# Two modulation chunks of the second layer computed at the end of the first layer's experts

## The chip, the cores and the metric

One core of a Trainium2 chip runs the whole program. The metric is the time of one execution in microseconds (us), as the device takes it. Names of engines are those of the profile: PE is the matrix engine and PEld its weight loads, DVE the vector engine, ACT the scalar engine, POOL the GpSimd engine, SP the engine that only issues transfers. A letter q behind an engine is its queue of issues.

## The reference, cut to what matters

Two layers act on 256 context rows and 512 latent rows of width 1024. Each layer makes six modulation vectors ("chunks" 0 to 5, 1024 numbers each) from a conditioning vector, once for the latent rows and once for the context rows:

```
m_lat = jnp.split((sc @ ada_w[i] + ada_b[i])[:, None, :], 6, axis=-1)
m_ctx = jnp.split(scc @ ada_w[i] + ada_b[i], 6, axis=-1)
h_lat = modulate(rms_norm(x, norm_mix_w[i]), m_lat[0], m_lat[1])
...
x = x + m_lat[2].astype(x.dtype) * y_lat
h_lat = modulate(rms_norm(x, norm_ffn_w[i]), m_lat[3], m_lat[4])
...
x = x + m_lat[5].astype(x.dtype) * f[B * L:].reshape(B, S, D)
```

`ada_w[i]` is 1024 by 6144 numbers of 4 bytes, so the weights of one chunk are 4 MB. They depend on nothing that the layers compute. The mixer between chunks 1 and 2 is softmax attention beside a gated delta rule that goes through the rows in 12 steps, forwards and backwards at once. The FFN is a mixture of 32 experts, two per row; each expert has 3 MB of weights.

## The kernel before, in words

Each layer goes through the same stages: norm and transposition of the rows (`norm_mix`, L424, in the second layer); the input projection, in units of columns, with the short convolution and the triangular solve of the delta rule (`layer`, L1593 on, in the order of `ORDER`, L126); the scan of 12 steps with the attention as filling (L1641); the output projection, norm and router (L1694); the experts (`experts`, L1421). A planner that simulates the program settles the order of the instructions on each engine and in each queue. Where `pin` (L163) is used, the order is that of the text.

**Modulation.** `ada_steps` (L271) makes one chunk in four parts; a part (`ada_part`, L257) loads 1 MB of `ada_w` by POOL's queue into one of two buffers (L231), multiplies it in eight matmuls of 128x32 by 128x256 on four column strips of PE (L265; the profile shows each as two records), and adds the result to a sum (ACT L267 for the first, DVE L269 for the others). After the fourth the bias is added (L282) and the chunk is written to a small array in DRAM, `md` (POOL's queue, L283). The scan calls a part for each letter a in `PAT` (L130), an attention slot for each f and a piece of the delta step for each d. In the second layer each of the 12 steps has two letters a, and there are 16 parts (chunks 2 to 5), so steps 0 to 7 have two each and the last four steps none. On PE the order of this stage is pinned.

**Experts.** Of an expert's weights, w1 and w3 (2 MB together) go into one of four buffers `w13` of 16 KB per partition (`RB`, L98; L1317), w2 into one of two buffers `w2`, all by SP's queue and three experts ahead (`LA`). Expert e multiplies in `expert_up` (L1362, L1364), turns the result (L1380), multiplies by w2 (L1406), scales (DVE L1413) and adds the rows into `yd` by an indirect transfer of POOL's (L1418). Each such addition waits for the one before it. After expert 31 there is a branch (L1503) for rows that overflow, and then the second layer begins: SP loads the rows x from `yd` (L1751), ACT squares them (L326), PE transposes (L343), `norm_chunks` makes the operands `nT`, `hh` and `hl` (L345 to L350).

**Memory.** The tiles of a stage lie in stacked pools. A tile that takes the place of older tiles waits until all work on those is done. In the second layer the pool "nm" of the norm begins with `nT` (24 KB per partition); when it closes, the pool "pp" of the projection begins at the same address with `gev` (L1558), which takes the first projected unit (c0 = 2560) from PSUM (`gate`, L1010). Three PSUM tiles of tag "a" hold such results (`PSA`, L111). In the first layer the `w13` buffers lie where the second layer has `hh`, `hl`, its first weights `wraw` (L231, the part on SP's queue) and the small table `wqk` (L444).

Of the kernel before, what the change touches and what calls it, by code (L numbers as in the profile page):

```python
# [13 lines left out]
F32 = mybir.dt.float32  # L14
# [115 lines left out]
PAT = (('fdfdfffdfffafddffffdfaffdfd', 'fdfffdffdfdfafddffdfafffdfaf', 'fdffdfffdfdfafddffdfafffdff'), ('fdffdffadffdfddafdffdf', 'fdffdffadffdfddafdffdf', 'fdffdffddadffdfadd'))  # L130
WB = 2
LA, E0 = 3, 2
QUEUE = dict(w="sync", ada="gpsimd", att="gpsimd", step="sync", idd="sync", iud="sync", ild="sync", iy="sync", ix="sync", qk="sync", qg="scalar", vk="scalar", h2="scalar", se="gpsimd", res="scalar")
# [11 lines left out]
class Model:  # L145
# [97 lines left out]
    def cond(self):  # L243
# [6 lines left out]
        nc.vector.tensor_scalar(cc, cc, 0.5, None, op0=OP.mult)  # L250
        sc = self.cp.tile([P, 8, 32], F32, name="scp")
        nc.vector.memset(sc, 0.0)
        nc.vector.scalar_tensor_tensor(sc[:, :, 0:2], th, 1.0, cc, op0=OP.add, op1=OP.mult)
# [17 lines left out]
    def ada_steps(self, i, ch, pool, q):  # L271
# [12 lines left out]
        yield  # L284

    def md_row(self, i, ch, v):

        return self.md[i][ch].rearrange("(o g r) j -> r o g j", o=1, g=4)[v].to_broadcast([P, 4, UNIT])

# [811 lines left out]
    def logit_shift(self, i, v, rw, rb, pool):  # L1101
# [3 lines left out]
        for g in range(4):  # L1105
            nc.sync.dma_start(m[32 * g:32 * g + 32], self.md[i][3][32 * g + v].rearrange("(p k) -> p k", k=8))
        mb = pool.tile([P, 8, P], F32, tag="h2T", bufs=1, name="mb")
# [202 lines left out]
    def expert_load(self, i, e, n, pool):  # L1310
# [13 lines left out]
        return w  # L1324

    def split(self, src, name, pool):

# [92 lines left out]

    def experts(self, i, R, js, g5, h2d, yd, ntok, xw):  # L1421

# [32 lines left out]
        def out(e):  # L1455
            if e >= 0:
                y = self.expert_out(py.pop(e), gates.pop(e), xp)
                self.expert_add(y, col(e), yd, ntok)
# [11 lines left out]
        eo, nb = R["eo"], R["nb"]  # L1470
        xes = []
        self.pins(True)
        for e in range(XE):
# [5 lines left out]
        for e in range(NE):  # L1479
            load(e + LA)  # L1480
            pa = self.psA("pab")
            xt, w, hl = x.pop(e), w13.pop(e), p13.pop(e)
# [13 lines left out]
        turn(NE - 1)  # L1496
        out(NE - 2)
        down(NE - 1)
        out(NE - 1)
        self.pins(False)  # L1500
        assert not list(rest)
# [21 lines left out]
    def layer(self, i, xsrc, rows, done, xstack, mod):  # L1523
# [20 lines left out]
        with self.pool("hp", B) as hp:  # L1544
            with self.pool("pj", B) as wp:
                mp.update(self.rope_params(i, wp))
                first = []
                with self.pool("nm", B) as pool:
                    start = lambda: first.extend(self.wnat(i, 2560, 288, wp))
                    hh, hl = self.norm_first(rows, start, pool, hp) if i == 0 else self.norm_mix(i, rows, start, mod, pool, hp)  # L1550
                done()
                mid = left.enter_context(self.pool("mid", A))
# [73 lines left out]
        with self.pool("at", B) as pool:  # L1626
# [3 lines left out]
            def modulation():  # L1630
                for l, ch in [(i, c) for c in range(2, 6)] + ([(i + 1, 0), (i + 1, 1)] if not last else []):
                    yield from self.ada_steps(l, ch, pool, QUEUE["ada"])
# [47 lines left out]
        nc.sync.dma_start(rb[:, 4:36], t["re_b"][i:i + 1, :].to_broadcast([P, 32]))  # L1680
        rt = self.route_open(T, rp)
        route = lambda n, lg: self.route_pair(rt, n, [tt - t0 for tt in tiles[n:n + 2]], lg, n == T - 2, tl)
        vb, vnow = {nm: tl.tile([P, D], F32, name=nm, tag=nm) for nm in ("g2", "m3", "s4")}, None
# [10 lines left out]
        for n, tt in enumerate(tiles):  # L1694
# [8 lines left out]
            if n == T - 1:  # L1703
                left.close()
                xw = xws.enter_context(self.pool("xw", A))
                ex = self.experts(i, rt, [tt - t0 for tt in tiles], g5, h2d, yd, ntok, xw)
                next(ex)
# [82 lines left out]
```

## Time and profile before

| what | value |
|---|---|
| time, median of 3 runs | 2092.97 us (2085.26 to 2104.73) |
| the profiled execution's own time | 2092.51 us |
| its span, first to last instruction | 2090.7 us |
| mean granted clock of PE, as a share of full speed | 0.902 |
| PE busy | 1763.9 us (84%) |
| DVE busy | 1460.2 us (70%) |
| ACT busy | 1016.6 us (49%) |
| POOL busy | 868.6 us (42%) |
| moved by DMA | 427.81 MB, mean 205 GB/s |

Busy time is the time in which an engine executes; shares are of the span. They are means over stages that have different limits, so the stages have to be read one by one. The experts of the first layer run from about 720 to 1104 us, the second layer's norm and projection from 1110 to about 1400, its scan from about 1460 to 1625, its experts at the end.

### The profile page before, as it was taken

To read this page: it belongs to the slowest core of one execution; us is meant where nothing else is said; L and a number is where in the kernel's file an instruction comes from. 1 tells how busy PE (TensorE), PEld (TensorE's weight loads), DVE (VectorE), ACT (ScalarE), POOL (GpSimd) and SP (SyncE) were. 2 spreads that over 40 slices of the span, in tenths; PEclk is the share of its full clock that TensorE was granted. 3 is DMA by queue.
4 is the path that set the end of the run, shared out by engine and by line. 5 is a ranking of instruction groups with operands and counts; after the bars stand their busy time and mean duration, and the time that the engine had idled before them with its cause. 6 is when DMAs were issued, how large, how long until landed. Compare 5 with 4: busy or idle time off the path is not lost. (4 is left out here: it accounts for less than half of the span.)

```text
span 2090.7 us, 35600 instructions
## 1 busy us (share of the span) xinstructions
PE 1763.9 (84%) x13835; PEld 1382.1 (66%) x13835; DVE 1460.2 (70%) x2472; ACT 1016.6 (49%) x1595; POOL 868.6 (42%) x915
## 2 busy tenths in 40 slices
PE   6998798978877879999996987776898577999994
PEld 4887687766656746666665866675676465777773
DVE  4469996567673668887874579992678465787774
ACT  3444344665541246565554543343566225666663
POOL 4456653234354423343226466650234443334321
PEclk9999897799998979999997998875899788999997
DMA  9222445798645389998853323445983558988872
GB/s 283 74 71 82 129 119 166 218 259 246 205 125 144 147 327 336 332 322 301 324 161 119 97 73 97 131 130 158 282 233 83 148 214 315 346 334 330 328 295 102
DMA packets 227687, 427.81 MB, mean 205 GB/s; under 512 B 83720, under 2 KB 157180, under 8 KB 202939
## 3 DMA queue, kind: packets, MB, share of 16 engines
q1 hardware_dynamic: 171547, 329.09, 47.1%
q0 software_dynamic: 33536, 72.59, 12.2%
q10 hardware_dynamic: 22432, 23.81, 3.3%
q8 instruction: 111, 1.82, 0.4%
q14 instruction: 61, 0.50, 0.1%
HBM read 386.82 MB, written 84.67 MB: 226 GB/s over the span
## 5 line engine op out<-in xcount | busy, mean ns | idle before, releaser
L1418 POOL DMA_INDIRECT yd<-ey,idx x64 | 114.2, 1784 | 425.3 <-DMA yd<-ey,idx 151.8
L1364 PE MATMUL pab<-w,xt 128*128 128x512 f32 x512 | 230.3, 592 | 0.0
L1332 ACT ACTIVATE w2h<-w 128x2048 fp32r<-128x2048 f32 x64 | 122.7, 1917 | 134.5 <-PE py L1406 83.3
L1333 DVE TENSOR_TENSOR w2l<-w,w2h 128x2048 fp32r<-128x2048 f32 x64 | 146.8, 2294 | 53.5 <-ACT w2h L1332 52.9
L1333 DVE TENSOR_TENSOR w13l<-w,w13h 128x2048 fp32r<-128x2048 f32 x64 | 146.5, 2288 | 28.9 <-ACT w13h L1332 28.9
L1364 PEld LDWEIGHTS pab<-w,xt 128*128 128x128 f32 x512 | 93.0, 191 | 92.0 <-issue 91.8
L489 POOL TENSOR_TENSOR wlo<-wraw,whi 128x1024 fp32r<-128x1024 f32 (+1 forms) x44 | 111.1, 2529 | 93.1 <-ACT whi L488 93.1
L239 PE MATMUL pn<-whi,hh 128*128 128x256 f32 (+1 forms) x432 | 134.6, 314 | 16.3 <-ACT gev L1562 12.5
L239 PE MATMUL po<-woh,m 128*128 128x512 f32 x320 | 114.1, 434 | 30.7 <-ACT woh L1069 14.5
L239 PE MATMUL pn<-whi,hl 128*128 128x256 f32 (+1 forms) x432 | 135.3, 316 | 2.0 <-DVE hl L350 1.7
L239 PE MATMUL pn<-wlo,hh 128*128 128x256 f32 (+1 forms) x432 | 132.4, 308 | 1.2 <-POOL wlo L489 1.2
L1332 ACT ACTIVATE w13h<-w 128x2048 fp32r<-128x2048 f32 x64 | 121.8, 1902 | 6.4 <-DMA w<-w 4.1
L239 PE MATMUL pt<-hh,wlo 128*128 128x512 f32 (+1 forms) x352 | 124.2, 353 | 0.0
L239 PE MATMUL pt<-hh,whi 128*128 128x512 f32 (+1 forms) x352 | 122.9, 349 | 0.0
L239 PE MATMUL pt<-hl,whi 128*128 128x512 f32 (+1 forms) x352 | 122.2, 347 | 0.0
L1406 PE MATMUL py<-w2h,gh 128*128 128x512 f32 x256 | 109.1, 426 | 4.6 <-DVE ey L1413 4.4
L1337 POOL DMA_INDIRECT xe<-h2d,idx x64 | 85.9, 1343 | 61.2 <-issue 22.9
L518 DVE SCALAR_TENSOR_TENSOR dT<-xin,cw,dT 128x772 f32<-128x772 f32 x64 | 80.1, 1252 | 43.3 <-ACT dT L516 41.5
L1406 PE MATMUL py<-w2h,gl 128*128 128x512 f32 x256 | 103.1, 403 | 7.8 <-DVE gl L1385 7.8
L1413 DVE TENSOR_TENSOR ey<-py,eg 128x1024 f32<-128x1024 f32 x64 | 78.2, 1222 | 44.1 <-PE py L1406 37.8
L239 PEld LDWEIGHTS pn<-whi,hh 128*128 128x128 f32 x432 | 90.6, 211 | 23.2 <-ACT gev L1562 13.5
L1348 PEld LDWEIGHTS xt<-cst,xe 128*128 128x128 f32 x512 | 68.3, 192 | 55.1 <-issue 29.8
(401 smaller groups left out, 5124.4 us busy)
## 6 DMA issues: line engine op xcount, KB each, us to landing
w<-w SPq DMA_DIRECT2D x192, 1024.0 KB, 9.8
araw<-ada_w POOLq DMA_DIRECT2D x40, 1024.0 KB, 6.8
wraw<-w_in SPq DMA_DIRECT2D x40, 512.0 KB, 4.1
lk<-vk SPq DMA_DIRECT2D x48, 256.0 KB, 7.2
lx<-xad SPq DMA_DIRECT2D x40, 256.0 KB, 10.0
araw<-ada_w SPq DMA_DIRECT2D x8, 1024.0 KB, 10.9
wr<-w_out SPq DMA_DIRECT2D x8, 1024.0 KB, 13.4
vk<-vr ACTq DMA_DIRECT2D x16, 384.0 KB, 3.7
```

Of the source, the lines that this page charges most:

```text
L239: self.nc.tensor.matmul(ps, a(k), b(k), start=(first and n == 0), stop=(last and n == 3 * nk - 1))
L489: getattr(nc, eng).tensor_tensor(lo, raw, hi, op=OP.subtract)
L518: nc.vector.scalar_tensor_tensor(dst, xin[:, tap:tap + 772], cw[:, tap, f:f + 1], dst, op0=OP.mult, op1=OP.add)
L1332: self.pin(nc.scalar.activation(hi, src, AF.Copy))
L1333: self.pin(nc.vector.tensor_tensor(lo, src, hi, op=OP.subtract))
L1337: self.pin(self.nc.gpsimd.indirect_dma_start(out=xe, out_offset=None, in_=h2d, in_offset=bass.IndirectOffsetOnAxis(ap=idx, axis=0), bounds ...
L1348: pin(nc.tensor.transpose(ps[:, k * P:(k + 1) * P], xe.rearrange("p (q k) -> p k q", k=8)[:, 4 * q + k, :], self.ident))
L1364: self.pin(self.nc.tensor.matmul(out, xt[:, k, :], w13[:, :, KS + k, :], start=False, stop=(k == 3)))
L1406: pin(self.nc.tensor.matmul(py[:, n * 512:(n + 1) * 512], a[:, j, :], b[:, c], start=(j + m == 0), stop=(j == 1 and m == 2)))
L1413: pin(nc.vector.tensor_tensor(y, py, gates, op=OP.mult))
L1418: self.pin(self.nc.gpsimd.indirect_dma_start(out=yd, out_offset=bass.IndirectOffsetOnAxis(ap=idx, axis=0), in_=y, in_offset=None, bounds_c ...
```

## The change

The second layer's chunks 2 and 3 (`LATE`) are no longer made in its scan. `experts` of the first layer gets a generator `ada_late`. It loads their 8 MB as four pieces of 2 MB (`half_load`, two transfers of 1 MB each on SP's queue) into `w13` buffers, where experts 32 to 35 would have come, one piece at each of the loop's last three turns and one behind it. Its 64 matmuls go to one PSUM tile: for the second chunk the vector operand is a shifted view of a padded tile (`self.scs`), so that its results fall into rows 2 and 3 of each strip. Eight of the matmuls stand ahead of expert 31's `expert_down` on PE, 56 behind it. ACT then copies the sum to a tile `la` in the pool "rp". In the second layer, `ada_close` opens a pool "lb" when "nm" has closed and before "pp" opens: it loads the two biases by SP's queue, adds them to the sum on DVE and writes two `md` arrays by POOL's queue. `md_row` and `logit_shift` read the second chunk two rows further down. The scan of the second layer has eight parts left (chunks 4 and 5), which fill the letters a of steps 0 to 3.

```diff
+LATE = (2, 3)
...
-        sc = self.cp.tile([P, 8, 32], F32, name="scp")
-        nc.vector.memset(sc, 0.0)
+        pad = self.cp.tile([P, 260], F32, name="scp")
+        nc.vector.memset(pad, 0.0)
+        self.scs = [pad[:, 2 - 2 * j:258 - 2 * j].rearrange("p (k r) -> p k r", k=8) for j in range(2)]
+        sc = self.scs[0]
...
+    def ada_late(self, i, chs, pool, load):
+        if not chs:
+            return
+        acc = self.late_sum = pool.tile([P, UNIT], F32, tag="la", name="la")
+        src = self.t["ada_w"][i].rearrange("(p k) n -> p k n", k=8)
+        raws = []
+        for ch in chs:
+            for n in range(2):
+                raws.append(load(src[:, 4 * n:4 * n + 4, ch * D:(ch + 1) * D]))
+                yield
+        ps = self.psC("aps")
+        for j in range(2):
+            for k in range(8):
+                if k % 2 == 0:
+                    yield
+                for g in range(4):
+                    w = raws[2 * j + k // 4][:, k % 4, g * UNIT:(g + 1) * UNIT]
+                    self.pin(self.nc.tensor.matmul(ps[32 * g:32 * g + 32, :UNIT], self.scs[j][:, k, :], w, start=(j + k == 0), stop=(j == 1 and k == 7), tile_position=(0, 32 * g)))
+        self.pin(self.nc.scalar.activation(acc, ps[:, :UNIT], AF.Copy))
+
+    def ada_close(self, i, chs, pool):
+        for j, ch in enumerate(chs):
+            ab = pool.tile([P, UNIT], F32, tag="lb%d" % ch, name="lb")
+            self.nc.sync.dma_start(ab, self.t["ada_b"][i, ch * D:(ch + 1) * D].rearrange("(g o j) -> g o j", g=4, o=1).to_broadcast([4, 32, UNIT]))
+            self.nc.vector.tensor_tensor(ab, self.late_sum, ab, op=OP.add)
+            getattr(self.nc, QUEUE["ada"]).dma_start(self.md[i][ch], ab)
+            self.mdrow[i, ch] = 2 * j
...
+    def half_load(self, src, pool):
+        w = pool.tile([P, 2, 8, FF], F32, tag="w13", bufs=RB, name="w13").rearrange("p a k f -> p (a k f)").rearrange("p (k n) -> p k n", k=4)
+        for n in range(2):
+            self.nc.sync.dma_start(w[:, 2 * n:2 * n + 2], src[:, 2 * n:2 * n + 2])
+        return w
...
         for e in range(NE):
             load(e + LA)
+            if e + LA >= NE:
+                next(late, None)
...
         turn(NE - 1)
         out(NE - 2)
+        for _ in range(3):
+            next(late, None)
         down(NE - 1)
         out(NE - 1)
+        for _ in late:
+            pass
...
                     hh, hl = self.norm_first(rows, start, pool, hp) if i == 0 else self.norm_mix(i, rows, start, mod, pool, hp)
+                if i > 0:
+                    with self.pool("lb", B) as lb:
+                        self.ada_close(i, LATE, lb)
                 done()
...
-                for l, ch in [(i, c) for c in range(2, 6)] + ([(i + 1, 0), (i + 1, 1)] if not last else []):
+                for l, ch in [(i, c) for c in range(2, 6) if i == 0 or c not in LATE] + ([(i + 1, 0), (i + 1, 1)] if not last else []):
```

## Rows read from the trace of the kernel before

**Rows 1.** The page's slices: GB/s in 40 equal parts of the span.
```profile
GB/s 283 74 71 82 129 119 166 218 259 246 205 125 144 147 327 336 332 322 301 324 161 119 97 73 97 131 130 158 282 233 83 148 214 315 346 334 330 328 295 102
```

**Rows 2.** Second layer's scan, DVE in time: start, duration, engine, line; one per step.
```profile
1520.37 0.68 DVE L921 TENSOR_TENSOR w<-pz,scs 128x512 f32<-128x512 f32 x1
1534.70 0.68 DVE L921 TENSOR_TENSOR w<-pz,scs 128x512 f32<-128x512 f32 x1
1550.92 0.68 DVE L921 TENSOR_TENSOR w<-pz,scs 128x512 f32<-128x512 f32 x1
...
1582.00 0.69 DVE L921 TENSOR_TENSOR w<-pz,scs 128x512 f32<-128x512 f32 x1
...
1593.72 0.68 DVE L921 TENSOR_TENSOR w<-pz,scs 128x512 f32<-128x512 f32 x1
```

**Rows 3.** Modulation parts on PE in time: one at half, one at full clock.
```profile
1417.33 1.94 PE L265 MATMUL aps<-araw,scp 128*32 128x256 f32 x16
...
1524.27 1.07 PE L265 MATMUL aps<-araw,scp 128*32 128x256 f32 x16
```

**Rows 4.** Windows, first experts' end: length, busy (x) of PE/PEld/DVE/ACT/POOL, PEclk, DMA, GB/s.
```profile
1040.00:1050.00 10.00, 10.00 (x43) 6.93 (x42) 9.96 (x9) 6.18 (x7) 3.10 (x2) 1.00 0.98 335
...
1070.00:1080.00 10.00, 9.54 (x41) 6.68 (x40) 9.96 (x9) 7.61 (x10) 1.57 (x1) 1.00 0.43 129
...
1090.00:1100.00 10.00, 7.79 (x27) 5.13 (x26) 4.42 (x7) 0.77 (x2) 3.45 (x2) 0.95 0.19 28
1100.00:1110.00 10.00, 2.97 (x8) 1.78 (x6) 1.42 (x2) 0.22 (x1) 3.47 (x9) 0.67 0.22 29
```

**Rows 5.** SP's queue in time, end of the first experts.
```profile
1061.00 11.21 SPq L1323 DMA_DIRECT2D w<-w  x2
...
1110.56 0.82 SPq L1751 DMA_DIRECT2D x<-yd  x2
```

**Rows 6.** Layer junction in time: PE's last product, last addition, first squares.
```profile
1098.16 0.47 PE L1406 MATMUL py<-w2h,gh 128*128 128x512 f32 x1 [2.21 <-DVE ey L1413]
...
1102.21 0.51 PE L1406 MATMUL py<-w2l,gh 128*128 128x512 f32 x1
...
1105.79 1.54 POOL L1418 DMA_INDIRECT yd<-ey,idx  x1 [5.96 <-issue]
...
1114.08 1.03 ACT L326 ACTIVATE sq<-x 128x1024 f32<-128x1024 f32 x1 [9.39 <-DMA x<-yd]
```

**Rows 7.** End of the second layer's norm in time, on POOL, ACT and PE.
```profile
1146.47 0.73 POOL L350 TENSOR_TENSOR hl<-nT,hh 128x256 fp32r<-128x256 f32 x1 [1.26 <-ACT hh L348]
...
1147.24 0.94 ACT L1010 ACTIVATE gev<-pn 128x256 f32<-128x256 f32 x3 [0.84 <-POOL hl L350]
...
1148.36 0.40 PE L239 MATMUL pn<-whi,hh 128*128 128x288 f32 x1 [0.70 <-ACT ba L1566]
```

**Rows 8.** DMA issues: output<-input, queue, count, KB each, median us to landing.
```profile
yl<-dy SPq DMA_DIRECT2D x24, 128.0 KB, 3.5
...
atd<-fu POOLq DMA_DIRECT2D x8, 256.0 KB, 5.3
...
ab<-ada_b POOLq DMA_DIRECT2D x10, 128.0 KB, 8.3
```

**Rows 9.** A chunk's last steps in the second scan, in time: bias addition and write.
```profile
1514.20 0.42 DVE L282 TENSOR_TENSOR ac<-ac,ab 128x256 f32<-128x256 f32 x1
...
1517.66 0.60 POOL L283 DMA_DIRECT2D md<-ac  x1
```

**Rows 10.** Windows as in Rows 4: the projection after the junction, and the solve.
```profile
1158.00:1168.00 10.00, 10.00 (x57) 8.77 (x56) 5.40 (x7) 4.47 (x8) 3.46 (x2) 1.00 0.55 157
...
1300.00:1400.00 100.00, 77.58 (x756) 68.77 (x754) 92.66 (x210) 33.79 (x67) 62.01 (x47) 0.86 0.37 107
```

**Rows 11.** Windows of 2 us, same columns, where PE starts again after an idle stretch.
```profile
1238.00:1240.00 2.00, 0.00 (x0) 0.00 (x0) 2.00 (x3) 1.37 (x3) 0.00 (x0) 0.75 0.12 40
1240.00:1242.00 2.00, 0.88 (x4) 0.88 (x5) 2.00 (x4) 1.78 (x2) 0.00 (x0) 0.50 0.00 0
...
1248.00:1250.00 2.00, 2.00 (x14) 2.00 (x14) 2.00 (x3) 0.96 (x4) 2.00 (x6) 0.69 0.78 281
```

More of the change, by code (lines that the diff above doesn't have):

```diff
@@ L250, in cond @@
         nc.vector.tensor_scalar(cc, cc, 0.5, None, op0=OP.mult)
-        sc = self.cp.tile([P, 8, 32], F32, name="scp")
-        nc.vector.memset(sc, 0.0)
+        pad = self.cp.tile([P, 260], F32, name="scp")
+        nc.vector.memset(pad, 0.0)
+        self.scs = [pad[:, 2 - 2 * j:258 - 2 * j].rearrange("p (k r) -> p k r", k=8) for j in range(2)]
+        sc = self.scs[0]
+        self.mdrow = {}
         nc.vector.scalar_tensor_tensor(sc[:, :, 0:2], th, 1.0, cc, op0=OP.add, op1=OP.mult)
@@ L284, in ada_steps @@
         yield
+    def ada_late(self, i, chs, pool, load):
[24 more added lines that the diff above has]
+            self.mdrow[i, ch] = 2 * j
     def md_row(self, i, ch, v):
-        return self.md[i][ch].rearrange("(o g r) j -> r o g j", o=1, g=4)[v].to_broadcast([P, 4, UNIT])
+        return self.md[i][ch].rearrange("(o g r) j -> r o g j", o=1, g=4)[v + self.mdrow.get((i, ch), 0)].to_broadcast([P, 4, UNIT])
     def mod_load(self, i, pool):
@@ L1105, in logit_shift @@
         for g in range(4):
-            nc.sync.dma_start(m[32 * g:32 * g + 32], self.md[i][3][32 * g + v].rearrange("(p k) -> p k", k=8))
+            nc.sync.dma_start(m[32 * g:32 * g + 32], self.md[i][3][32 * g + v + self.mdrow.get((i, 3), 0)].rearrange("(p k) -> p k", k=8))
         mb = pool.tile([P, 8, P], F32, tag="h2T", bufs=1, name="mb")
@@ L1419, in expert_add, with experts @@
                                                    bounds_check=ntok - 1, oob_is_err=False, compute_op=OP.add))
-    def experts(self, i, R, js, g5, h2d, yd, ntok, xw):
+    def experts(self, i, R, js, g5, h2d, yd, ntok, xw, late):
         nc, tc = self.nc, self.tc
@@ L1471, in experts @@
         xes = []
+        late = self.ada_late(min(i + 1, DEPTH - 1), late, R["pool"], lambda src: self.half_load(src, xw))
         self.pins(True)
@@ L1681, in layer @@
         rt = self.route_open(T, rp)
+        rt["pool"] = rp
         route = lambda n, lg: self.route_pair(rt, n, [tt - t0 for tt in tiles[n:n + 2]], lg, n == T - 2, tl)
@@ L1705, in layer @@
                 xw = xws.enter_context(self.pool("xw", A))
-                ex = self.experts(i, rt, [tt - t0 for tt in tiles], g5, h2d, yd, ntok, xw)
+                ex = self.experts(i, rt, [tt - t0 for tt in tiles], g5, h2d, yd, ntok, xw, () if last else LATE)
                 next(ex)
```

## The prediction

> **What bounds the kernel now.** I read the slices first, to see where transfers have room, then four stretches that the change touches. In the slices the reader sees two plateaus above 300 GB/s, the two expert stages, and between them lower figures [rows 1]. So memory traffic is a bound in the experts and not elsewhere, and a change that carries 8 MB from the second scan to the end of the first plateau has to be read in both places.
>
> The second scan comes next. Its steps are marked by one DVE instruction each; from step 4 to step 8 there are 1582.00 - 1520.37 = 61.6 us, and the eight parts that go are the last eight of the sixteen, all in steps 4 to 7 [rows 2]. The order on PE is pinned, so every part stands in the way of what follows it.
>
> Then the end of the first experts. The load is 335 GB/s at 1040 to 1050, and 28 to 29 GB/s at 1090 to 1110, while PE is busy to about 1095 [rows 4]: the weights of expert 31 are in, and some 35 us follow in which DMA is nearly free. The chain there goes over PE's last product (to 1102.7), the last addition to `yd` at 1105.79, the loads of x at 1110.56 and the squares at 1114.08 [rows 5, 6].
>
> Last, the junction of norm and projection. `gev` starts on ACT at 1147.24, released by the last `hl` on POOL, and PE, which had filled its three PSUM tiles, goes on at 1148.36 [rows 7]. Right behind, PE is busy without a gap, 10.00 of 10 us at full clock, and later DVE with 92.66 of 100 us [rows 10]. A delay at 1148 has nothing beside it that could absorb it: it moves the projection, then the solve, then the end.
>
> **Removed: eight parts in the second scan.** A part takes PE 1.07 us at full clock [rows 3]; eight of them are 8.6 us, the least that goes. The steps say more. The interval 1534.70 to 1550.92 holds three parts and ten attention slots and lasts 16.2 us; 1582.00 to 1593.72 has the same letters without the three parts and lasts 11.7 us [rows 2]. That is 1.5 us per part, the wait for its 1 MB included, so eight parts are **-12.0 us**. The upper end is four intervals of 11.7 us, 46.9 instead of 61.6: -14.7 us. I take the middle, as it comes from two intervals with equal letters. The eight loads with their issues on POOL, the sums on ACT and DVE, two bias loads and two writes go as well, off the chain. What follows the scan waits for its results, so the gain stays.
>
> **Added at the end of the first experts.** The first two pieces can start when SP has issued its last `w2` load, at 1072.2 (1061.00 + 11.21, [rows 5]); the other two wait until experts 30 and 31 have read their buffers, to about 1093. Eight MB at 335 GB/s [rows 4] are 25 us, so they end at about 1102. They cost expert 31 nothing, whose weights are ahead in the queue. They run beside expert 30's addition to `yd`, for which expert 31's waits (it stood idle 5.96 us, [rows 6]): up to 3 us. On PE the first eight matmuls fit into the 2.21 us in which PE waits for DVE [rows 6]. The other 56, seven parts' worth, follow the last product: 7 times 1.07 is 7.5 us at full clock, 7 times 1.94 is 13.6 us at half [rows 3], so they end between 1110 and 1116. ACT copies the sum ahead of its squares, which begin at 1114.08 [rows 6]: 0 to 3 us late. The cover is the wait for the last addition and the loads of x. These two delays overlap; against them PE may be left at a higher clock than the 0.67 of 1100 to 1110 [rows 4], worth a us or two at the start of the norm. Ends -2 and +4; I take **+2 us**, since each delay has a row that shows its place and the gain has none. On SP's queue the two `wqk` loads and the loads of x stand behind the pieces; the former now wait for a piece's buffer until about 1105, still ahead of 1110.56. The matmuls and the sum themselves cost nothing else.
>
> **Added at the junction.** The bias tiles of "lb" lie where `nT` lay, and `gev` lies on both. So the bias loads wait for the last `hl`, and `gev`, which today starts at once behind that `hl` [rows 7], waits until both `md` writes have landed. Nothing hides this chain: second issue on SP about 0.4 us behind the first; landing 3.5 us, by the nearest row of that size and queue, `yl`; addition 0.42 us; two issues on POOL of 0.60 us; landing of a write [rows 8, 9]. For the write the nearest row is `atd`, the same queue and direction, 5.3 us at twice the size under load; here DMA is light, so I take 3.5 again. The sum is 0.4 + 3.5 + 0.42 + 1.2 + 3.5 = 9.0 us. With 2.5 us for each landing, an estimate below `yl`, it is 7.0; with 8.3 us for the bias and 5.3 for the write it is 15.6 [rows 8]. Behind the waiting `gev` on ACT stand the copies that free the PSUM tiles, behind these PE. PE's idle before 1148.36 is lost today too, so about **+8.4 us** reach it.
>
> PE then starts cold. After an idle stretch of about 5 us it runs at 0.50 at 1240 and is back only at about 1249 [rows 11]; some 7 busy us at half speed lose **+3.4 us** in a stretch where PE is the bound. Ends 0 and 4.
> The Trainium skill (TensorE: Matmul & The Clock Gate, "HAM oscillation — how this bites in real kernels") says that a wait for data between groups of matmuls puts the array back to its slow clock and that the next group starts cold, which speaks against this change; the trace agrees at 1240, with 0.50.
> The Trainium skill (DMA: Bandwidth & Descriptors, "Anatomy of one DMA — SWDGE (gpsimd) path") gives a small transfer a fixed cost of about 2.0 us, mostly the receipt of the write; by it each landing would be an estimated 2.3 us, the chain 6.6 instead of 9.0, and the time 2.4 us less than below; the rows here lie above that figure, with 3.5.
>
> Padding `scp` and reading `md` two rows further down cost nothing: no instruction more.
>
> **Sum.** -12.0 + 2 + 8.4 + 3.4 = +1.8 us on the profiled execution's 2092.5 us (span 2090.7, 1.8 around it), which stands 0.5 under the median shown: **2094 us**. No change that can be measured.
>
> **Rivals.**
> *The write-back is hidden.* If the planner finds PE other work, or the wait of `gev` is served early, the junction costs nothing: -12.0 + 2 = -10, 2082 us. For it: the biases and the sum are ready long before 1147. Against it: three PSUM tiles stand full, and `gev` today starts within 0.1 us of the last `hl` [rows 7]. Chance 0.2.
> *The write-back is long: slower.* On POOL's queue the two writes stand behind other work of the projection, and the bias lands as late as the 8.3 us row [rows 8]. Then the junction takes 15.6 us, PE loses 4, the first experts' end 4, and the scan gives only the 8.6 us of its matmuls: +15, 2107 us. It decides from the point where the junction with its cold start takes more than the 10 us that scan and experts' end leave. For it: no work hides any us of it. Against it: DMA is at a low share there. Chance 0.15.
> *The tail does not hold the eight MB.* If the pieces come late (the clock stays at half, the last piece lands after 1105), the sum ends past 1118 and ACT's squares, `wqk` and `hh` wait: 5 us more, 2099 us. The slack of 1102 against 1114 speaks against it [rows 6]. Chance 0.1.
> That the chunks would not move at all is excluded by the edit.
>
> **Chances and range.** The forecast has 0.55. Its own range, from 8.6 to 14.7 for the scan and 7 to 11 for the junction, is 2086 to 2102. The runs shown lie up to 12 us from their median, and 1%, 21 us, is about what separates a change from none here. To leave out no more than 2 in 10 the range takes in the hidden write-back and most of the long one: **2080 to 2107 us**. Faster by over 1% would need the hidden write-back and a scan gain beyond 14.7 us at once: 0.06. Slower by over 1% needs the long write-back and a lost gain at once: 0.08. Within 1%: 0.86.
>
> **What would show it.** In the changed trace: steps 4 to 8 of the scan 12 us shorter, with no modulation matmul behind step 3; GB/s near 300 from about 1072 to 1102; modulation matmuls behind the last product, ended before the squares; between the last `hl` and `gev` two bias loads, two additions and two writes, some 8 us, PE idle meanwhile and at 0.50 behind it. The prediction is wrong if `gev` follows the last `hl` without that gap, if the scan shortens by less than 8 us, or if the squares start over 5 us later than after expert 31 today.

## The result, and the profile after

The changed kernel takes **2115.78 us** (median of 8 runs, 2111.47 to 2123.63) against 2093.25 (8 runs) for the kernel before: a ratio of **1.0105, 95% interval 1.0076 to 1.0134**. It is slower by 22.5 us, where I forecast 2094 and a range up to 2107. Its profiled execution has a span of 2114.1 us, 23.4 above that of before, and a mean granted clock of 0.891.

I cut both executions at the same instructions: the first addition to `yd` of the first experts (before at 772.17), the first squares (1114.08), the first product `gr` behind the projected gates on DVE (1153.31), the first, fifth and eleventh `w` of the second scan (1465.04, 1520.37, 1611.22), the end. The columns below are the stretches between these marks, in us, each from one profiled execution; the later rows are the experiments, told further down, with their ratio to before (medians of several runs).

| kernel | experts | junction | solve | scan 1st-5th `w` | scan 5th-11th | to the end | ratio (interval) |
|---|---|---|---|---|---|---|---|
| before | 341.9 | 39.2 | 311.7 | 55.3 | 90.9 | 479.5 | |
| after | 348.2 | 49.6 | 315.9 | 56.1 | 90.5 | 481.1 | 1.0105 (1.0076-1.0134) |
| e1_scan_only | 340.8 | 40.0 | 311.9 | 56.4 | 91.1 | 491.7 | 1.0030 (1.0011-1.0049) |
| e2_tail_only | 347.2 | 40.0 | 312.8 | 59.1 | 94.2 | 481.5 | 1.0059 (1.0033-1.0086) |
| e3_junction_only | 340.4 | 49.9 | 316.5 | 54.4 | 93.8 | 482.3 | 1.0083 (1.0052-1.0115) |
| e4_lb_aside | 349.7 | 39.4 | 316.1 | 57.1 | 87.3 | 478.8 | 1.0054 (1.0030-1.0078) |
| e5_close_early | 351.0 | 40.2 | 314.6 | 60.5 | 88.2 | 481.1 | 1.0049 (1.0027-1.0072) |
| e6_parts_twice | 341.9 | 40.0 | 311.7 | 56.9 | 94.1 | 489.0 | 1.0057 (1.0034-1.0081) |
| e7_loads_only | 346.9 | 39.3 | 316.9 | 57.9 | 94.2 | 479.9 | 1.0078 (1.0050-1.0106) |
| e8_one_chunk | 340.8 | 39.3 | 316.3 | 58.1 | 87.6 | 479.0 | 1.0013 (0.9993-1.0032) |
| e9_four_memsets | 340.9 | 39.2 | 311.3 | 55.8 | 93.9 | 478.6 | 0.9988 (0.9963-1.0012) |
| e10_five_memsets | 339.4 | 40.2 | 314.0 | 53.2 | 91.4 | 479.3 | 1.0004 (0.9980-1.0028) |
| e11_parts_no_loads | 341.2 | 40.0 | 314.7 | 57.9 | 92.4 | | scan only |
| e12_no_parts | 338.5 | 40.0 | 307.6 | 40.7 | 90.1 | | scan only |
| e13_letters_later | 341.3 | 40.0 | 307.3 | 42.7 | 99.0 | 481.7 | **0.9963 (0.9946-0.9979)** |
| e14_changed_later | 348.4 | 51.4 | 312.6 | 41.1 | 91.8 | 485.3 | 1.0051 (1.0029-1.0073) |
| e15_one_chunk_later | 342.0 | 39.3 | 314.8 | 43.0 | 99.8 | 485.0 | 1.0024 (1.0006-1.0042) |
| e16_first_no_loads | 341.3 | 40.0 | 315.0 | 45.4 | 90.6 | | scan only |

After less before: +6.3, +10.4, +4.1, +0.8, -0.4, +1.6, and +0.6 ahead of the first mark: 23.4. I had put +2, +11.8, nothing, -12 for the scan, nothing.

**The transfers** (page, GB/s in 40 slices, answering to [rows 1]): slices 20 and 21 show the 8 MB, 241 and 124 for 161 and 119; slices 29 and 30, the second scan, are 108 and 71 for 233 and 83.
```profile
GB/s 280 77 82 78 118 114 176 242 227 237 201 134 136 201 310 348 322 332 300 329 241 124 90 76 110 93 172 113 265 108 71 143 210 316 342 330 330 318 302 97
```

**First experts' end** (windows, columns as in [rows 4]). DMA share is now 0.72 to 0.87 where it fell to 0.43 and 0.19, and PE works the sums at nearly full clock.
```profile
1070.00:1080.00 10.00, 10.00 (x43) 7.16 (x42) 8.33 (x9) 6.12 (x8) 2.06 (x1) 1.00 0.72 247
1080.00:1090.00 10.00, 10.00 (x43) 7.16 (x42) 8.53 (x9) 6.32 (x8) 1.70 (x1) 1.00 0.87 313
1090.00:1100.00 10.00, 8.79 (x45) 5.44 (x44) 5.32 (x7) 1.14 (x4) 1.54 (x1) 1.00 0.75 237
1100.00:1110.00 10.00, 7.65 (x119) 4.35 (x117) 1.42 (x2) 0.60 (x2) 1.54 (x1) 0.99 0.33 60
```
SP's queue (answering to [rows 5]): the late pieces do not wait for the last `w2`. The first goes at 1058.23, the second at 1072.82, each ahead of a `w2` load.
```profile
1058.23 0.89 SPq L1365 DMA_DIRECT2D w<-ada_w  x2
1060.42 0.34 SPq L1358 DMA_DIRECT2D w<-w  x1
1072.82 0.88 SPq L1365 DMA_DIRECT2D w<-ada_w  x2
1073.81 0.41 SPq L1358 DMA_DIRECT2D w<-w  x1
1082.88 10.94 SPq L1365 DMA_DIRECT2D w<-ada_w  x4
...
1116.98 0.80 SPq L1804 DMA_DIRECT2D x<-yd  x2
```
The additions on POOL, the late matmuls, their copy and the squares in time (answering to [rows 6]; in brackets the idle time before, and what ended it). The additions follow each other by 10.6, 10.4, 9.0 and 7.9 us; before, the last four steps were 7.7, 7.4, 9.9 and 7.5, and the 9.9 were no wait for the addition ahead: expert 30's addition waited there for its rows `ey` from DVE. The matmuls and the copy end at 1107.9, 13 us ahead of the squares: they are not what is late. First two additions of before, then the rows of after:
```profile
1088.39 3.52 POOL L1418 DMA_INDIRECT yd<-ey,idx  x1 [5.46 <-DVE ey L1413]
1098.29 1.54 POOL L1418 DMA_INDIRECT yd<-ey,idx  x1 [6.38 <-DVE ey L1413]
```
```profile
1074.16 2.06 POOL L1460 DMA_INDIRECT yd<-ey,idx  x1 [8.58 <-issue]
1084.77 1.70 POOL L1460 DMA_INDIRECT yd<-ey,idx  x1 [8.55 <-DMA yd<-ey,idx]
1095.17 1.54 POOL L1460 DMA_INDIRECT yd<-ey,idx  x1 [8.70 <-DVE eu L1414]
1104.16 1.54 POOL L1460 DMA_INDIRECT yd<-ey,idx  x1 [7.45 <-DMA yd<-ey,idx]
1112.06 1.54 POOL L1460 DMA_INDIRECT yd<-ey,idx  x1 [6.35 <-issue]
...
1101.16 6.25 PE L309 MATMUL aps<-w,scp 128*32 128x256 f32 x112
...
1107.48 0.38 ACT L310 ACTIVATE la<-aps 128x256 f32<-128x256 f32 x1 [10.98 <-PE aps L309]
...
1120.93 1.03 ACT L361 ACTIVATE sq<-x 128x1024 f32<-128x1024 f32 x1 [11.72 <-DMA x<-yd]
```

**Junction** (answering to [rows 7, 9]). The last `hl` ends at 1154.83; then two bias loads, two additions, two writes, and `gev` at 1162.72: 7.9 us of wait where there were none, and PE idle for 8.56.
```profile
1154.10 0.73 POOL L385 TENSOR_TENSOR hl<-nT,hh 128x256 fp32r<-128x256 f32 x1 [1.26 <-ACT hh L383]
...
1154.86 1.31 SPq L316 DMA_DIRECT2D lb<-ada_b  x2
...
1158.60 0.43 DVE L317 TENSOR_TENSOR lb<-la,lb 128x256 f32<-128x256 f32 x1 [4.70 <-DMA lb<-ada_b]
...
1160.61 0.56 POOL L318 DMA_DIRECT2D md<-lb  x1 [0.58 <-DVE lb L317]
...
1162.72 0.94 ACT L1045 ACTIVATE gev<-pn 128x256 f32<-128x256 f32 x3 [8.70 <-DMA md<-lb]
...
1163.84 0.61 PE L240 MATMUL pn<-whi,hh 128*128 128x288 f32 x1 [8.56 <-ACT ba L1618]
```
The windows behind it (answering to [rows 10, 11]) show PE busy without a gap. The clock of 0.71 in the first is a mean of two levels: windows of 2 us show 0.50 (1.2 GHz) up to about 1168 and 1.00 (2.4 GHz) from there.
```profile
1162.00:1172.00 10.00, 8.16 (x49) 8.14 (x50) 2.91 (x7) 4.31 (x12) 5.84 (x6) 0.71 0.01 3
1172.00:1182.00 10.00, 10.00 (x57) 8.73 (x56) 4.67 (x7) 5.00 (x8) 5.18 (x3) 1.00 0.56 159
```
```profile
1164.00:1166.00 2.00, 2.00 (x9) 2.00 (x10) 0.22 (x1) 0.32 (x2) 1.74 (x3) 0.50 0.00 0
...
1168.00:1170.00 2.00, 2.00 (x19) 2.00 (x18) 0.42 (x1) 1.07 (x3) 1.74 (x1) 1.00 0.00 0
```

**Scan** (the `w` marks, answering to [rows 2]). Fifth to ninth take 58.2 us for 61.6; but sixth to seventh, three parts fewer, take 13.1 for 16.2, and ninth to tenth, which had no part before either, 14.0 for 11.7.
```profile
1542.56 0.69 DVE L956 TENSOR_TENSOR w<-pz,scs 128x512 f32<-128x512 f32 x1 [1.31 <-PE pz L952]
1557.89 0.69 DVE L956 TENSOR_TENSOR w<-pz,scs 128x512 f32<-128x512 f32 x1
1571.02 0.69 DVE L956 TENSOR_TENSOR w<-pz,scs 128x512 f32<-128x512 f32 x1
...
1600.81 0.67 DVE L956 TENSOR_TENSOR w<-pz,scs 128x512 f32<-128x512 f32 x1
1614.76 0.69 DVE L956 TENSOR_TENSOR w<-pz,scs 128x512 f32<-128x512 f32 x1 [0.31 <-PE pz L952]
```

### The profile page after: what moved, and what is told of

It reads as the page before. It is cut to its first block, busy times and chain, and to the rows that moved or that the text cites. A ratio compares the mean times of both kernels' runs of the same rounds, so it can differ in the third digit from the quotient of the medians.

```text
span 2114.1 us, 35590 instructions
## 1 busy us (share of the span) xinstructions
PE 1782.0 (84%) x13835; PEld 1398.0 (66%) x13835; DVE 1458.1 (69%) x2466; ACT 1016.5 (48%) x1594; POOL 862.4 (41%) x905
## 5 line engine op out<-in xcount | busy, mean ns | idle before, releaser
L1375 DVE TENSOR_TENSOR w2l<-w,w2h 128x2048 fp32r<-128x2048 f32 x64 | 147.4, 2303 | 56.1 <-ACT w2h L1374 53.2
L1406 PEld LDWEIGHTS pab<-w,xt 128*128 128x128 f32 x512 | 93.1, 191 | 92.0 <-issue 91.8
L240 PEld LDWEIGHTS pn<-whi,hh 128*128 128x128 f32 x432 | 91.4, 213 | 26.2 <-ACT ba L1618 12.1
L1404 PE MATMUL pab<-w13h,xth 128*128 128x512 f32 x256 | 104.4, 408 | 0.5 <-ACT xth L1392 0.5
## 6 DMA issues: line engine op xcount, KB each, us to landing
araw<-ada_w POOLq DMA_DIRECT2D x32, 1024.0 KB, 10.2
```

Of the source, the lines that this page charges most:

```text
L240: self.nc.tensor.matmul(ps, a(k), b(k), start=(first and n == 0), stop=(last and n == 3 * nk - 1))
L1375: self.pin(nc.vector.tensor_tensor(lo, src, hi, op=OP.subtract))
L1404: self.pin(self.nc.tensor.matmul(out, a[:, k, :], b[:, :, k, :], start=(k + m == 0), stop=False))
L1406: self.pin(self.nc.tensor.matmul(out, xt[:, k, :], w13[:, :, KS + k, :], start=False, stop=(k == 3)))
```

## Experiments: one part of the change at a time

**Scan alone.** `ada_late` is not called; `md_row` and `logit_shift` read chunks 2 and 3 from the first layer's `md`.
```diff
+        return self.md[0 if ch in LATE else i][ch]...
-    ex = self.experts(..., () if last else LATE)
+    ex = self.experts(..., ())
```


> The kernel before with the eight parts taken out of the second layer's scan and nothing put in their place: where chunks 2 and 3 of the second layer are read, those of the first layer are read instead, so the values differ. Theory A (read from the trace after): the scan's length is set by the pinned chain of attention slots between PE, ACT and DVE, and the parts lay in gaps of it; then 0 to -4 us. Theory B (the prediction): each part costs 1.5 us of the scan; then -12 us, -8.6 to -14.7.


The scan took 147.5 us, for 146.2 before, at a mean clock of 0.93 for 0.97: nearer to A. With other values the router chooses other experts, and the second experts' additions span 318.9 us for 309.3, so only the scan is read from it. The 12 us that I had forecast did not come.

**Experts' end alone.** Loads, matmuls and copy are added, the scan keeps its sixteen parts, nobody reads the sum; against the changed kernel:
```diff
-                        self.ada_close(i, LATE, lb)
-... (i, c) for c in range(2, 6) if i == 0 or c not in LATE ...
+... (i, c) for c in range(2, 6) ...
```


> The kernel before with the late loads, the 64 matmuls and the copy of the sum at the end of the first experts, the sum not used; the second layer's scan still makes all its chunks. Theory A: the additions to yd form a chain in which each waits for the one before to land, and the 8 MB slow several of them; the loads of x start 6 to 7 us later than before, and the time is +6 to +8 us. Theory B (the prediction): only the last but one addition is slowed, +2 us (-2 to +4).


Experts +5.3, above the 2 us of my sum and nearer to A. The whole is 12 us slower, more than either theory had; in the profiled execution the scan, unchanged in its text, took 153.2 us for 146.2 (clock 0.93 for 0.97): a first sign that one scan is no measure.

**Junction alone.** The kernel before with the two bias loads, additions and writes, into spare arrays.
```diff
+            self.nc.vector.tensor_tensor(ab, ab, ab, op=OP.add)
+            ...dma_start(self.dr.tile([P, UNIT], F32, name="spare%d" % ch), ab)
```


> The kernel before with the pool between norm and projection alone: two bias loads, two additions (each bias to itself) and two writes to spare arrays; nothing late, the scan as before. Theory A and the prediction agree on the wait (gev 8 to 9 us behind the last hl); the prediction puts the cold start of PE at 3.4 us more, +11.8 us together; if the stretch from gev to the scan loses more than that, as the trace after suggests (gev 15.5 us late, the first step of the scan 21.4 us late), +14 us.


Junction +10.7, as in the changed kernel; solve +4.8, which no theory had. The whole is 17 us slower, above the 14 of the highest theory.

**Biases aside.** The changed kernel with "lb" on the other side of the memory, opened ahead of the norm.
```diff
+                    with self.pool("lb", A) as lb:
+                        self.ada_close(i, LATE, lb)
                     hh, hl = ... self.norm_mix(...)
-                    with self.pool("lb", B) as lb:
-                        self.ada_close(i, LATE, lb)
```


> The changed kernel with the pool lb on the other side of the memory and opened ahead of the norm, so that bias loads, additions and writes run while the norm loads its rows and gev waits for nothing new. Theory A: what is left is the late end of the first experts, 6 to 8 us over the kernel before, and 14 us less than the changed kernel. Theory B (the scan gives 12 us back, the junction cost 12): 8 to 12 us less than the changed kernel too, but then below the kernel before if the experts' end costs only 2: -10 us.


The junction is back at 39.4, and the time 10 us below the changed kernel's; it is still 11 us above before, where A had 6 to 8. The edit moves "lb" in place and in time at once. That `gev` waited for the writes is in its row above (`<-DMA md<-lb`), and it reads nothing of them; so the shared address is the reason left, and the wait is gone with it. Solve still +4.4.

**Early close.** Biases in pool "rp", one addition on DVE straight from PSUM, one `md` write at the end of the experts.
```diff
-        self.pin(self.nc.scalar.activation(acc, ps[:, :UNIT], AF.Copy))
+        self.pin(self.nc.vector.tensor_tensor(ab, ps[:, :UNIT], ab, op=OP.add))
+        getattr(self.nc, QUEUE["ada"]).dma_start(self.md[i][chs[0]], ab)
```


> The changed kernel with the junction emptied: the biases lie in the first layer's pool 'rp' and are loaded behind the last piece, DVE adds them straight from PSUM (no copy on ACT), and the one md write goes out at the end of the first experts instead of behind the last hl. Theory A (the wait of gev for the md write is a real 8 us, the 8 MB delay the additions to yd, the scan gives next to nothing, and the solve has the changed kernel's order on DVE, 4 us longer than before): gev starts within 0.5 us of the last hl; squares 3 to 7 us later than before; gate to first scan step +4; scan -3 to 0: about +4 to +8 against before, 2098 to 2102 us, ratio 1.002 to 1.004, some 12 us better than the changed kernel. Theory B (what I predicted: the scan gives 12 us and the junction eats it): -12 + 2, about 2083 us, ratio 0.995. Theory C (the junction is hidden elsewhere and something else made the change slow): no better than the changed kernel, 2113 us or more.


`gev` follows the last `hl` (ACT, in time) and the junction is 40.2. The ratio is 1.0049, above A's 1.002 to 1.004: the experts' end cost 9 us here, where A had 3 to 7.
```profile
1151.75 0.94 ACT L1044 ACTIVATE gev<-pn 128x256 f32<-128x256 f32 x3 [0.84 <-POOL hl L384]
```

**Loads only.** As the experts' end alone, without the 64 matmuls and the copy.
```diff
-                    self.pin(self.nc.tensor.matmul(ps[32 * g:32 * g + 32, :UNIT], ...))
-        self.pin(self.nc.scalar.activation(acc, ps[:, :UNIT], AF.Copy))
```


> The scan as before; at the first experts' end the four pieces of 2 MB are loaded as in the changed kernel and nothing reads them (no matmuls, no sum). Theory A (the 8 MB alone stretch the chain of additions to yd from 7.5 to 10 us each): squares 3 to 6 us later than before, like the kernel with loads and matmuls. Theory B (the matmuls behind the last product, or the lower clock, make the end late): squares within 1 us of before. In both, the second layer's solve may take the other order that the changed kernel has, 4 us more from gate to first scan step; so the whole is +6 to +10 by A and 0 to +5 by B.


Experts +5.0, the same as with the matmuls: A. (The whole, +16 us, is above A's 6 to 10; the profiled execution is the fastest of the five.) The additions on POOL lie 10.6 and 10.2 us apart while the pieces are loaded.
```profile
1067.52 1.93 POOL L1450 DMA_INDIRECT yd<-ey,idx  x1 [8.77 <-issue]
1078.10 1.60 POOL L1450 DMA_INDIRECT yd<-ey,idx  x1 [8.65 <-DMA yd<-ey,idx]
1088.26 1.54 POOL L1450 DMA_INDIRECT yd<-ey,idx  x1 [8.56 <-DVE eu L1404]
```

**One chunk.** The early close with 4 MB, twelve parts left in the scan.
```diff
-LATE = (2, 3)
+LATE = (2,)
```


> As the early close (no wait at the junction), but only chunk 2 is made at the first experts' end: 4 MB, two pieces, 32 matmuls; the second scan keeps twelve parts. Theory A (chain of additions): half the transfers, so the squares only 1 to 3 us later than before; solve in the changed kernel's order, +4; scan -1.5 to 0: +3 to +6, about 2098 us. Theory B (1.5 us of scan per part): -6 for four parts, +1 at the experts' end: 2088 us. Theory C (a tail is all or nothing, because any late load stands ahead of the loads of x): squares as late as with 8 MB, +4 to +6.


Experts 340.8, and 342.0 with the same 4 MB in e15: four MB cost nothing that shows, eight cost 5 to 9. Counted from the first mark (773.22 here), two additions are 2.6 and 2.1 us later than before, and the next, expert 30's, is 1.1 us earlier. Before, it waited for `ey` from DVE; here it waits for the addition ahead. So the chain of additions has slack at that one place, which takes the delay of 4 MB and not that of 8:
```profile
1084.67 1.54 POOL L1458 DMA_INDIRECT yd<-ey,idx  x1 [8.80 <-DVE w13l L1373]
1091.58 1.68 POOL L1458 DMA_INDIRECT yd<-ey,idx  x1 [5.37 <-DVE w2l L1373]
1098.29 1.54 POOL L1458 DMA_INDIRECT yd<-ey,idx  x1 [5.03 <-DMA yd<-ey,idx]
1105.44 1.54 POOL L1458 DMA_INDIRECT yd<-ey,idx  x1 [5.61 <-DVE wqk L479]
```

## Experiments: the solve's order

`sY` of the solve is written out three times on SP. In the kernel before that is 196, 242 and 268 us behind the product `gr`; in the changed kernel 207, 234 and 272. The planner puts DVE's steps in another order, and it does so in e3, e4, e5, e7, e8 as well. Two kernels differ from before by memsets of a spare tile alone, and by one of them from each other:
```diff
+                if i > 0:
+                    with self.pool('zz', A) as zz:
+                        z = zz.tile([P, 256], F32, tag='z', name='zz')
+                        nc.gpsimd.memset(z, 0.0)   # four or five times
```


> The kernel before with four memsets of a spare 128x256 tile on POOL behind the second layer's norm; the solve keeps on DVE the order of the kernel before. It is the partner of the next kernel. All theories: gate to first scan step 312 us, the whole within 0.2% of before. Its scan, with all sixteen parts, shows how much the same scan differs from run to run: theory A (the granted clock differs, 0.93 to 0.97 in the scans so far) first to eleventh w 146 to 153 us, short where the clock is high; theory B (the scan before is fixed by its pinned order) 146 to 147 us again.

> As the last kernel with one memset more; with it the planner puts the solve's steps on DVE in the order that the changed kernel has (the first of its three results about 11 us later, the third 4 to 6 us later). Theory A (that order is what costs the changed kernel 4 us between gate and scan): S to first w 316 us instead of 312, squares and gate as before, the whole +3 to +5, ratio 1.0015 to 1.0025. Theory B (those 4 us come of the late start, the clock or the memory, not of the order): 312 us, ratio 1.000.


With four, `gr` is at 1158.52 and the writes (SP in time, first and third) at +196.3 and +268.3:
```profile
1354.80 0.32 SPq L826 DMA_DIRECT2D dy<-sY  x1
...
1426.86 0.33 SPq L826 DMA_DIRECT2D dy<-sY  x1
```
With five, `gr` is at 1147.61 and they are at +207.7 and +272.5:
```profile
1355.29 1.09 SPq L826 DMA_DIRECT2D dy<-sY  x1
...
1420.10 0.33 SPq L826 DMA_DIRECT2D dy<-sY  x1
```
The stretch is 311.3 and 314.0: +2.7 in the solve, between A's 316 and B's 312. The two ratios overlap, so no loss of the whole is shown. The scans of the pair, equal in their text, are 149.7 and 144.7 us.

## Experiments: what a part of the scan costs

**Matmuls twice** for the eight parts in steps 4 to 7 of the kernel before.
```diff
-        for r in range(2):
+        for r in (range(2) if i == 0 or ch < 4 else (0, 1, 0, 1)):
```


> The kernel before with the eight matmuls of each part of chunks 4 and 5 done twice in the second scan (steps 4 to 7); no load more, the result is the same. 8 times 1.07 = 8.6 us of PE more between the fifth and the ninth w. Theory A (PE is the bound of these steps at 92% busy, but the attention's chain over ACT and DVE leaves gaps that take part of it): from the fifth to the ninth w 61.6 becomes 65 to 70, the whole +4 to +8. Theory B (the order on PE is pinned, every part's product is on the path in full): +8.6 or more, and the steps behind do not give it back. Theory C (the parts lie wholly in gaps of the attention's pace): 0 to +2.


Fifth to ninth `w` 64.0 for 61.6, fifth to eleventh 94.1: +3.2 against before's profile, but within the 90.9 to 94.2 of scans with sixteen plain parts. B is out, and A's 65 to 70 was not reached. The whole is 12 us slower, most of it behind the scan (489.0 for 479.5): from the eleventh `w` to the first addition of the second experts it takes 156.8 us for 148.1. The cause stays open.

**Without loads** for the same eight parts.
```diff
-        raw = self.wload(...)
+        if i == 0 or ch < 4:
+            self.kept = self.wload(...)
+        raw = self.kept
```


> The kernel before, but the parts of chunks 4 and 5 (the eight in steps 4 to 7 of the second scan) multiply the weights of the last part of chunk 3 again, without loads of their own: these two chunks come out with other values, so the second layer's router chooses other experts and only the scan is read. Theory A (a part costs its load's wait more than its matmuls: doubling the matmuls added about 1 us): from the fifth to the eleventh w 87 to 90 us, as without the eight parts, where with them 91 to 94 were seen. Theory B (the matmuls are the price, 8 times 1.07): 91 to 94 us, as with parts. Theory C (of my prediction, 1.5 us per part of which 0.43 is the wait): 3.4 us less than with them.


92.4: among those with loads, so A is out. In steps 4 to 7 the loads cost nothing that shows.

**No part at all.** e1 with `LATE = (2, 3, 4, 5)`.


> The kernel before without any part in the second scan: chunks 2 to 5 of the second layer are read from the first layer's, so its values and its experts differ and only the scan is read. Theory A (the attention's chain over ACT and DVE sets the pace, parts lie beside it for the most part): first to eleventh w 139 to 145 us, 0.3 to 0.5 us per part less than with sixteen. Theory B (1.5 us per part): 24 us less, 122 to 128 us. Theory C (PE alone, 1.07 us per part): 17 us less, 129 to 133 us.


130.8 us: less than A allowed. It lies in C's range by luck, as C takes 1.07 us for every part, and the fall is not even: first to fifth `w` fell by 14.6 us, fifth to eleventh stayed at 90.1. Windows (first to fifth, fifth to eleventh) of the kernel before and of this one: DMA share 0.93 to 0.75, clock 0.91 to 1.00.
```profile
1465.04:1520.37 55.33, 46.71 (x645) 34.53 (x646) 36.64 (x75) 30.15 (x58) 16.90 (x20) 0.91 0.93 274
1520.37:1611.22 90.85, 80.70 (x1328) 63.52 (x1328) 70.96 (x148) 59.74 (x112) 30.83 (x34) 1.00 0.62 173
```
```profile
1464.11:1504.82 40.71, 34.07 (x513) 27.02 (x514) 31.93 (x65) 28.07 (x55) 8.48 (x8) 1.00 0.75 212
1504.82:1594.88 90.06, 77.67 (x1215) 64.44 (x1215) 68.64 (x140) 58.94 (x110) 26.47 (x27) 0.93 0.35 89
```

**First eight without loads.** Parts of chunks 2 and 3 multiply the first one's weights.


> The kernel before, but the eight parts of chunks 2 and 3 (steps 0 to 3 of the second scan) all multiply the weights of the first of them, so seven of eight loads are gone and all matmuls stay: these two chunks come out with other values, so the second layer's router chooses other experts and only the scan is read. Theory A1 (in steps 0 to 3 the price of a part is its load): first to fifth w 42 to 48 us. Theory A2 (it is the matmuls on PE's pinned order): 52 to 56, as before. If both have a share, it lies between, and the rest of the 15 us is the matmuls'.


45.4 us: of the 14.6 us, 9.9 go with the seven loads; the other 4.7 are the matmuls' and those of the loads that are kept. The waits of PE agree: between these marks PE waits for the weights of parts three times in the kernel before (in all, times, longest, us), and not once here.
```profile
PE aps L265 <- DMA araw<-ada_w: 7.8, 3, 3.5
```

**The changed kernel with its parts in steps 4 to 7**, and the same edit on the kernel before and on e8.
```diff
-                    for c in PAT[i][s % 3]:
+                    for c in PAT[i][s % 3] if i == 0 or s >= 4 else PAT[i][s % 3].replace("a", ""):
```


> The changed kernel with its eight remaining parts in steps 4 to 7 instead of 0 to 3; nothing else. Theory A (place): first to fifth w 41 to 46 us instead of 56, from the fifth to the eleventh 91 to 94 instead of 90; the scan 10 to 14 us shorter than the changed kernel's, the whole 2102 to 2108 us, still above before by the 8 us of the experts' end, the 10 of the junction and the 3 to 4 of the solve's order. Theory B (parts cost the same wherever): 2115, as the changed kernel.


The scan is 132.8 us, 13.8 less than in the changed kernel with as many parts: A. That it is about the gain I had forecast is luck: it comes from where the parts stand, not from their number. 4 us of it were lost again behind the scan (485.3 for 481.1). Windows as above:
```profile
1485.04:1526.10 41.06, 35.23 (x529) 27.61 (x530) 31.80 (x64) 28.95 (x56) 9.26 (x9) 1.00 0.76 210
1526.10:1617.87 91.77, 82.26 (x1332) 64.48 (x1333) 73.29 (x150) 60.97 (x114) 31.33 (x34) 1.00 0.57 160
```


> The kernel before with its sixteen parts moved inside the second scan: no letter a in steps 0 to 3, so two parts in each of steps 4 to 11; the result is the same. Theory A (a part costs nearly 2 us in steps 0 to 3, where the scan's own loads share a memory that is busy at 0.93, and 0.4 us in steps 4 to 7): first to fifth w 41 to 46 us instead of 55, the eleven w together 134 to 140 instead of 146, and what follows the scan 0 to 3 us later for the last parts: the whole -5 to -12, ratio 0.994 to 0.9975. Theory B (sixteen parts cost the same wherever they stand): no change, ratio 1.000. Theory C (the memory is only moved: the loads of the output weights from step 4 on collide instead): first to fifth w shorter, the rest longer by as much, 0 to +4.


2084.88 us, ratio 0.9963: faster than both kernels without moving anything out of the scan. The parts in steps 8 to 11 take back 8 of the 12.6 us; the solve, in which the first part of before stands (the 1417.33 of [rows 3]), gives 4.4 more.


> The kernel with only chunk 2 made early (4 MB at the experts' end, closed at once), and its twelve parts in steps 4 to 9 of the scan. Theory A (place; 4 MB at the experts' end cost nothing): e8's 2097.5 less 10 to 14 for steps 0 to 3, plus up to 3 for the parts in steps 8 and 9: 2084 to 2090 us, ratio 0.995 to 0.998; about as good as the kernel before with its letters moved, as the four parts less are worth only 1 to 2 us and the solve's order costs as much. Theory B: 2097, as e8.


A was wrong: 1.0024, no better than e8. Against e8 the first steps give 15.1 us, but the later ones take 12.2 and the time behind the scan 6.0; twelve parts behind step 4 cost as much there as sixteen (99.8 and 99.0). Of the 12.2, 4.9 are one wait: ahead of the eleventh `w` PE waits for `lk`, whose last addition stands on DVE behind a reduction of finished rows that waits for ACT.
```profile
1605.79 0.69 DVE L1056 TENSOR_REDUCE oss<-o 128x8 f32<-128x512 f32 x1 [2.20 <-ACT o L1054]
...
1607.26 0.68 DVE L943 TENSOR_TENSOR lk<-lk,yt 128x512 f32<-128x512 f32 x1
```
```profile
1607.99 2.04 PE L950 MATMUL pz<-lk,lx 64*64 64x64 f32 x32 [4.92 <-DVE lk L943]
```
The rest, and the 6.0 us behind the scan, stay open.

## Why the prediction was wrong, by its steps

Two of the three signs that the prediction names for being wrong came: the scan did not shorten by 8 us, and the squares start 6.9 us later. The wait of `gev`, the third, was there.

**The scan, -12: mis-sized, and it decided the sign.** Fifth to eleventh `w` took 90.9 to 94.2 us, mean 93.1, in six executions with sixteen plain parts (before, e2, e3, e7, e9, e10), and 87.3 to 91.1, mean 89.3, in four without the last eight (after, e1, e4, e5). That is 3.8 us, about 0.5 per part, and between the two single profiles only 0.4. In both groups the stretch is by and large longer where the mean clock is lower: with the parts 90.9 at 1.00 and 94.2 at 0.96, without them 87.3 at 0.99 and 91.1 at 0.93. At the same 0.97, e3 has 93.8 and e5 88.2. So at equal clock the parts are worth about 4 to 6 us, a third to a half of my 12, and the pair shows none of it because before's execution had 1.00 and after's 0.95.

Four things failed in the step. "A part costs 1.5 us" came from neighbouring intervals with equal letters [rows 2]. The one with three parts, once these were gone, took 13.1 to 16.6 us in five executions (after, e1, e4, e5, e12), and never the 11.7 of its neighbour; why the neighbour is short is open, since it took 14.0 in after but 11.7 again in e4. Next, "the order on PE is pinned, so every part stands in the way of what follows it" does not hold where PE then waits for something else: between fifth and ninth `w` PE waits 4.6 us for ACT's softmax (`pp`) in after, 1.4 in before, and even twice the matmuls changed little. Third, I priced the parts as alike, while those between the first and the fifth `w` cost 13 to 15 us together (e12, e13, e14). That "memory traffic is a bound in the experts and not elsewhere" was a wrong reading that hid this: in that stretch the DMA share is 0.93, at 274 GB/s. Last, the marks: the interval from the fifth to the ninth `w` holds seven of the eight parts that go; the eighth stands just ahead of it.

**The experts' end, +2: mis-sized.** It took 6.3 in this pair; six executions with 8 MB lie at 346.9 to 351.0 and ten with none at 338.5 to 341.9, a difference of the means (348.6 and 340.8) of 7.8. The delay that I named, an addition slowed by the transfers, was right, but I let it touch one addition, and the pieces are not all behind the last `w2`. Three or four additions in a row stay at the 10 us of the loaded stage instead of its quiet end's 7.5: those that start from 1066 to 1085 take 8.9 to 11.2 us to land in e2, e4, e5 and e7, with 8 MB beside them, and 6.1 to 8.0 in e1, e3 and e6 without. The matmuls, on which I spent most of the working, cost nothing, as forecast; e7 shows it.

**The junction, +8.4 and +3.4: right in mechanism, a little high in size.** 7.9 us of wait at `gev`, 8.56 at PE, where I had 9.0 for the chain; the first load took 3.7 us to its addition, the last write 2.1 from its issue. PE's 0.70 us of idle before, which I took off the chain, stayed: 8.56 is about 0.7 more than the new wait. PE's cold start cost 1.8 us from `gev` to `gr` (7.8 for 6.1) rather than 3.4: the clock was 0.50 as forecast, but PE worked at it for about 4 us and not 7. The other 0.8 of the 10.4 lie ahead of the last `hl`. The Trainium skill (DMA: Bandwidth & Descriptors, "Anatomy of one DMA — SWDGE (gpsimd) path") gives about 2.0 us of fixed cost for a transfer on POOL's path. The write on POOL's queue, 2.1 us to its waiter, agrees; the load, 3.7 us, went by SP's queue, which that section is not about. The prediction's estimate by it, 6.6 us for the chain, is below the 7.9 measured. The Trainium skill (TensorE: Matmul & The Clock Gate, "HAM oscillation — how this bites in real kernels") says that matmuls behind a wait for data start cold; the 0.50 behind 8.56 us of wait agrees.

**The solve, +4.1: not in my sum.** The planner took another order on DVE; e10 against e9 shows 2.7 us with it in that stretch. Of the kernels that work on parts ahead of the scan, the seven with before's order take 311.3 to 315.0, mean 312.7, and the seven with the other 314.0 to 316.9, mean 315.8. But the clock goes along with it: the five at 0.81 and 0.82 take 311.3 to 312.8, all of before's order, and the nine at 0.79 and 0.80 take 314.0 to 316.9, among them e11 and e16, which have before's order. Against the clock alone speak e13 and e14, without parts ahead and both at 0.81: 307.3 with before's order, 312.6 with the other. So the order has a share of its own; how large it is beside the clock's is open.

**Rivals.** The slow rival came nearest in time (2107) and for the wrong reason: the junction was not long; its other two clauses, a smaller scan and a longer experts' end, were what happened, both further than its bounds. The hidden write-back is refuted by the 7.9 us in the changed kernel and by e3, the tail that does not hold the 8 MB by the copy at 1107.48.

## What to carry to other kernels

Before work is moved out of a stage, find where in the stage it costs: the same kind of part was worth about 2 us where the DMA share was 0.93 (14.6 us for eight in e12, 12.6 for seven in e13, the clock that rose with it included) and 0.5 to 0.8 where it was 0.75, and moving the parts within the stage gave more than moving half of them out. Do not price a removed step by a neighbouring interval without it; the neighbour may be short for another reason. A chain of waiting transfers at the quiet end of a loaded stage is on the path, and enough background load there slows each link; look for the place where the chain has slack, since a delay smaller than that costs nothing.

## What I had not expected of the hardware

The same pinned scan, text unchanged, took 144.7 to 153.2 us in six executions; the mean clock in it was 0.98 in the shortest and 0.93 in the longest, and those scans, taken alone, differ by more than the change is worth. Four MB beside the additions cost nothing that shows, eight 5 to 9 us against before's profile. Half-rate stretches go with PE's waits: between first and fifth `w` the mean clock is 0.86 to 0.95 in the executions whose parts wait there for their weights, and 0.96 to 1.00 in those (e12 to e16) with at most one part there, or with the loads gone.
